# Compressed keys' block sums: plain 4 KB gathers through the shared ring, added on chip, in place of 1 KB gathers that add in SBUF

## The chip, the cores and the metric

The kernel runs on one core of a Trainium2 chip. Its time is device microseconds of one launch, from start to end, and a version is judged by the median of its runs. The engines are TensorE (PE, with its weight load PEld), VectorE (DVE), ScalarE (ACT), GpSimd (POOL) and SyncE (SP, which here only issues DMAs). DMA moves data on 16 engines that share the queues of SP and POOL.

## What is computed

One step of a two-layer decoder (model width 1024) for a prompt of 512 tokens and for 8 samples of one token each. The samples look back on 2048 cached tokens, which lie in pages of 128 rows, in an order that a page table gives. Each layer has a mixer and a squared-ReLU feed-forward (1024 to 4096 and back); all weights are shared by prompt and samples. The mixer has three groups of heads: forgetting attention ("fox"), native sparse attention ("NSA") and a multi-scale pooling.

The change is in the samples' compressed branch of NSA. It takes the means of the cached k_cmp and v_cmp over blocks of 64 rows, scores the query against the 32 means, and those scores also select the blocks that the selected branch reads next. A row of this cache holds four vectors, of which the branch needs the first two: 256 of 512 floats.

```
cache_nsa_kv (DEPTH, N_POOL_PAGES, PAGE_SIZE, 4, KV_NSA, HEAD_DIM)   # [k_cmp, v_cmp, k_sel, v_sel]

def _cmp_branch(q5, qpos, kc_rows, vc_rows):
    def blocks(r):                                   # CMP_BLOCK = 64
        rb = r[:, :nbc * CMP_BLOCK].reshape(b, nbc, CMP_BLOCK, KV_NSA, HEAD_DIM)
        return jnp.mean(rb.astype(f32), axis=2).astype(r.dtype)
    kc, vc = blocks(kc_rows), blocks(vc_rows)
    s = jnp.einsum('btkgd,bnkd->btkgn', q5, kc) * SCALE
    ...
    p = _masked_softmax(s, mask)
    o = jnp.einsum('btkgn,bnkd->btkgd', p.astype(vc.dtype), vc)
    return o, jnp.sum(p, axis=3)                     # the sum ranks the blocks to select
```

There are 8 samples x 32 blocks = 256 blocks in each layer, two halves of 128 blocks. One block lies on one partition.

## The kernel before

**How work is put in order.** The program is written as chains, Python generators that emit a piece of work at a time and say what it weighs. `merge` (L118) always takes the chain that is furthest behind, by emitted weight over the chain's total (`W_G`, `W_S`, `W_C0`, `W_C1` and so on, L26). A chain that waits for another's result steps aside. Then the Tile framework's scheduler gives each engine a fixed order of instructions when the program is built, by priorities and by the order of emission. On the chip an engine goes through its order and cannot pass an instruction that waits.

**The main chain.** `main` (L1522) goes through each layer's dense products, all by `next_gemm`: a product of a 128 x 128 weight tile with up to 512 columns of activations is done as three fp32r products, hi x hi, hi x lo and lo x hi (`pg`, L336). Weights come as 256 KB tiles `wr` through SP and are split in `wh` and `wl` by ACT and DVE. The feed-forward runs in NC = 8 chunks, each with four tiles of ff1 and eight of ff2. Chunks 0 to 3 hold the prompt's columns alone. Chunks 4 to 7 are joint: their columns hold the samples too, and they are emitted only once the samples' chain is "joined".

**The samples' chain.** `sample` (L1466) goes first through the fox heads: per layer 64 gathers `fk` of 768 KB, on POOL's queue, each multiplied by the queries (L1204), summed, and multiplied with the weights on PE (`pvf`, L1212). Then `key_sample`, a unit per sample, gathers window keys `kt` and selected keys `st`: `psb` (L1122) are its small products, `pvw` and `pvs` (L1418) those with the values. The selected rows come from `ixs`, which `nsa_sample` (L1294) works out after it has waited for `kct`, the transposed means. Then `rows_of` multiplies the samples' rows by whole weight rows, `wrow` tiles of 512 KB through SP, four `prw` products (L268) each: 8 tiles of the output projection, then for SQ = 2 quarters 8 tiles of ff1 and 8 of ff2, 40 in all. Between them stand the samples' norms (`psr`). After the last of these rows comes "joined".

**The ring.** `ring` (L180) gives big tiles out of one rotation of RING = 5 buffers of 768 KB, in order of emission. `fk`, `kt`, `st` and `wrow` go through it. A tile's load can start when the fifth tile before it has been read. `take` (L1161) loads up to five ahead.

**The compressed sums.** `pre_cmp` (L631) sums while it gathers. For each half g and each row r of 64, one indirect DMA on POOL's queue brings 256 floats (1 KB) for each of 128 blocks, and from the third row on it adds them to what stands in SBUF (`compute_op` add). Two accumulators a half (CA = 2) take turns:

```
L637  G.indirect_dma_start(out=ys[g][r % CA], out_offset=None, in_=nsav,
                           in_offset=bass.IndirectOffsetOnAxis(ap=idxc[:, l, g:g + 1], axis=0),
                           element_offset=r * 512, compute_op=OP.bypass if r < CA else OP.add)
```

These 128 tiles `cg` a layer have buffers of their own. Then DVE adds the two accumulators and scales, PE transposes (`pkc`), and `kct` is there. Layer 0's sums are the chain `cmp0`, from the start of the layer, beside the mixer. Layer 1's are emitted during layer 0 by `fill` (L1640) once layer 0's NSA samples are done.

Of the kernel before, what the change touches and what calls it, by code (L numbers as in the profile page):

```python
# [34 lines left out]
def constants():  # L35
# [44 lines left out]
    c["ph"], c["p64"], c["p8"], c["p8x8"] = 128.0 * (p % 2)[:, None], 2.0 * (p % 64)[:, None], (p % 8)[:, None], 8.0 * (p % 8)[:, None]  # L80
# [57 lines left out]
def trunk(ctx: ExitStack, tc: tile.TileContext, x_prompt, x_sample, cache_fox_kv, cache_fox_logf, cache_nsa_kv,  # L138
# [44 lines left out]
    # ---------------------------------------------------------------- weight stream  # L183
# [15 lines left out]
    # the output projection in two halves: the features that come first, then the NSA heads'  # L199
# [64 lines left out]
    def row_mm(acc, rows, k, hk, raw, first, last):  # L264
        """A weight tile of 128 rows, 512 columns times up to 32 rows of activations, fp32."""
        for c in range(2 * hk, 2 * hk + 2):
          with PF():
            PE.matmul(acc[c * 32:(c + 1) * 32, 0:256], rows[:, k, :], raw[:, (c % 2) * 256:(c % 2 + 1) * 256],  # L268
                      start=first, stop=last)

    def row_end(sb, tag):
        """The sums feature-major: [128, f, c, 32] holds feature tile 2 c + f."""
# [8 lines left out]
    def ada(l, parts, tag, raws=None, hold=True):  # L281
        """Parts of a layer's modulation, from c's columns; hold: a PSUM bank is held for all of a part's tiles."""
# [27 lines left out]
    def next_gemm(kind, mhi, mlo, evac, cols, tag="g"):  # L310
        """The stream's next weight tile times the given ranges of columns."""
# [7 lines left out]
        for o in range(2 if two else 1):  # L319
            nk = 4 if two else 8  # L320
            for a, b in cols:
                acc = ps("pg", tag)
                if it[2] == "fg":
                    # 24 outputs alone, in fp32: a quarter of the features to each column group
# [18 lines left out]
    # ---------------------------------------------------------------- x and c  # L343
# [20 lines left out]
    # the first two parts' weights in what is free at the start  # L364
# [41 lines left out]
    # ---------------------------------------------------------------- vectors  # L406
# [21 lines left out]
    # ---------------------------------------------------------------- constants on chip  # L428
# [24 lines left out]
    # ---------------------------------------------------------------- page indices  # L453
# [5 lines left out]
    for l in range(L):  # L459
        t = ring("ti", (128, 2))  # L460
        V.tensor_copy(t, pgc)
        V.tensor_scalar(t, t, 256.0, C("ph"), op0=OP.mult, op1=OP.add)
        V.tensor_scalar(idxc[:, l], t, float(l * NPOOL * 256), None, op0=OP.add)
# [14 lines left out]
    nsav = cache_nsa_kv.rearrange("l n r (t2 t) k d -> (l n r t2) (t k d)", t2=2)  # L478

# [4 lines left out]
    # ---------------------------------------------------------------- norms  # L484
# [9 lines left out]
    def squares(X, fresh=None, then=None):  # L494
        """The prompt's squares of X summed over the features, on all partitions. fresh(k) brings tile k up to date, and
        then(k) reads it."""
# [11 lines left out]
    def pre_scaled(l, X, gi, sp, bp, fresh, tag, ph=None):  # L508
        """The prompt's X * g * (1 + scale), split, and 1 / rms(X), which is left for the products to take. The shift is
        the operand's column T (and the next, as these are even in number). ph: the squares, if they are there."""  # L510
# [27 lines left out]
    def post_norm(X, O, acc, pool=True):  # L538
        """The update X += rms(O) tile by tile, for O with its gates and acc the squares summed over the feature tiles."""
# [19 lines left out]
    def gated(O, gg, acc, m, src, a, b):  # L559
        """Columns a..b of O's tile m: the squares of src into acc, src times its gates to O."""  # L560
# [11 lines left out]
    def s_rms(x):  # L572
        """1 / rms of the samples' columns x [128, 8, 8], on all partitions."""
# [8 lines left out]
    def s_post(l, gi, gp, x):  # L582
        """XS += rms(x) * g * gate."""
# [8 lines left out]
    def s_pre(l, gi, sp, bp, out, rs=None):  # L592
        """out = rms(XS) * g * (1 + scale) + shift."""
# [9 lines left out]
    def s_put(hi, lo, x):  # L603
        """The samples' columns of an operand."""
# [7 lines left out]
    # ---------------------------------------------------------------- what a layer's samples need of the caches alone  # L612
# [18 lines left out]
    def pre_cmp(l):  # L631
# [35 lines left out]
    def layer(l, X, hi, lo, rsw):  # L667
# [972 lines left out]
        def fill():  # L1640
# [4 lines left out]
            for _ in pre_cmp(l + 1):  # L1645
                yield 0.25
# [81 lines left out]
```

## Time and profile before

| | |
|---|---|
| runs, us | 2087.47, 2085.21, 2074.53 |
| median, us | 2085.21 |
| profiled execution, span, us | 2088.8 |
| its mean granted clock of TensorE | 0.903 |

The profile is of one execution. Its span runs from the first instruction to the last, and the page gives no launch time beside it, so that the span stands for that execution's time. It lies 3.6 us above the median of the three runs, which is no more than they differ from each other.

The page shows each engine's busy time as a sum over the span and in 40 slices of 52.2 us. "PE 1888.1 (90%) x13848" is busy time, share of the span and number of instructions. Below are three rows of the 40 slices, in tenths: POOL's busy share, the clock that TensorE was granted, and the busy share of the 16 DMA engines.

```profile
POOL 0788888878888887100000254553435455000000
PEclk9998985696988888999999999975789999999998
DMA  8988888876988867786334666653337466684332
```

Slices 1 to 11 are layer 0's mixer, 12 to 21 its feed-forward, 22 to 31 layer 1's mixer and 32 to 40 its feed-forward. POOL is nearly full up to the 16th slice, in the middle of layer 0's feed-forward, and then idle until layer 1's mixer. DMA is near 0.8 as long, and about half as busy in layer 1's mixer.

A group row of the page reads: line, engine, operation, out<-in by the program's names (partitions x elements), number of instructions | busy time in us, mean of one in ns | idle time of the engine just before them, and what ended most of it.

### The profile page before, as it was taken

What the parts mean: (1) busy time and instruction counts of PE and PEld (TensorE: products, weight loads), DVE (VectorE), ACT (ScalarE), POOL (GpSimd) and SP (SyncE); (2) the same over time, 40 slices, a digit from 0 to 9 for tenths busy, and PEclk for the clock granted to TensorE, in tenths of its full rate; (3) what the DMA queues carried; (4) which work ended last, traced back from release to release, by engine and by line L of the source; (5) the groups of instructions that cost most, each with busy time, mean ns of one, the idle gap of its engine ahead of it and who ended that gap; (6) DMA issues with size and microseconds to landing.
All of it is one profiled execution on the core that took longest, in us unless ns stands there. A gap on an engine that the chain in (4) does not pass through costs nothing. (4 is left out here: it accounts for less than half of the span.)

```text
span 2088.8 us, 37062 instructions
## 1 busy us (share of the span) xinstructions
PE 1888.1 (90%) x13848; PEld 1475.4 (71%) x13848; DVE 1253.2 (60%) x3064; ACT 856.8 (41%) x1994; POOL 946.5 (45%) x670
## 2 busy tenths in 40 slices
PE   6987976998876888999998999979998989999998
PEld 3866753465545678779996777755665778879998
DVE  3557665665573357634557668786557967534555
ACT  3333332455442223323446344344555533324445
POOL 0788888878888887100000254553435455000000
PEclk9998985696988888999999999975789999999998
DMA  8988888876988867786334666653337466684332
GB/s 285 277 200 226 218 202 226 222 216 110 263 208 199 218 165 194 245 296 213 92 92 127 180 218 201 206 168 126 115 107 233 138 183 182 194 279 140 89 90 77
DMA packets 333687, 387.42 MB, mean 185 GB/s; under 512 B 30489, under 2 KB 267771, under 8 KB 333364
## 3 DMA queue, kind: packets, MB, share of 16 engines
q1 hardware_dynamic: 272324, 233.24, 36.4%
q0 software_dynamic: 61184, 151.82, 27.8%
q8 instruction: 110, 1.80, 0.4%
q14 instruction: 69, 0.57, 0.1%
HBM read 363.71 MB, written 21.44 MB: 184 GB/s over the span
## 5 line engine op out<-in xcount | busy, mean ns | idle before, releaser
L336 PE MATMUL pg<-ah,wh 128*128 128x262 f32 (+4 forms) x1792 | 549.4, 308 | 32.1 <-DVE rl L1570 9.7
L336 PE MATMUL pg<-ah,wl 128*128 128x262 f32 (+4 forms) x1792 | 544.0, 304 | 8.6 <-DVE wl L245 6.8
L336 PE MATMUL pg<-al,wh 128*128 128x262 f32 (+4 forms) x1792 | 544.1, 305 | 4.7 <-DVE al L522 4.5
L637 POOL DMA_INDIRECT cg<-in_cache_nsa_kv_dram,idxc x256 | 423.6, 1655 | 88.4 <-issue 68.9
L178 ACT ACTIVATE wh<-wr 128x512 fp32r<-128x512 f32 x372 | 234.0, 630 | 458.1 <-PE pg L336 416.5
L336 PEld LDWEIGHTS pg<-ah,wh 128*128 128x128 f32 x1792 | 351.4, 197 | 58.8 <-issue 32.5
L336 PE MATMUL pg<-a,wh 128*128 128x262 f32 (+3 forms) x1664 | 380.5, 317 | 11.6 <-DVE F L1589 7.0
L336 PEld LDWEIGHTS pg<-ah,wl 128*128 128x128 f32 x1792 | 351.9, 196 | 29.3 <-issue 11.6
L336 PEld LDWEIGHTS pg<-al,wh 128*128 128x128 f32 x1792 | 350.6, 196 | 28.4 <-issue 11.0
L245 DVE TENSOR_TENSOR wl<-wr,wh 128x512 fp32r<-128x512 f32 x368 | 276.2, 751 | 130.0 <-ACT wh L178 127.0
L336 PEld LDWEIGHTS pg<-a,wh 128*128 128x128 f32 x1664 | 278.2, 192 | 41.4 <-DVE F L1589 10.8
L336 PE MATMUL pg<-a,wl 128*128 128x258 f32 (+3 forms) x832 | 260.6, 314 | 0.9 <-DVE wl L245 0.9
L481 POOL DMA_INDIRECT fk<-in_cache_fox_kv_dram,idxf x128 | 131.8, 1030 | 276.7 <-PE pvf L1212 114.8
L1204 POOL TENSOR_TENSOR fk<-fk,qb 128x768 f32<-128x768 f32 x96 | 186.5, 1961 | 118.4 <-DMA fk<-in_cache_fox_kv_dram,idxf 58.1
L336 PEld LDWEIGHTS pg<-a,wl 128*128 128x128 f32 x832 | 160.0, 192 | 8.9 <-DVE wl L245 1.4
L1589 DVE TENSOR_TENSOR F<-F,pg 128x262 f32<-128x262 f32 (+3 forms) x188 | 88.3, 474 | 113.7 <-PE pg L336 108.7
L1205 DVE TENSOR_REDUCE S<-fk 128x12 f32<-128x768 f32 x128 | 120.6, 944 | 43.9 <-POOL fk L1204 43.4
L1626 POOL TENSOR_TENSOR xt<-xt,yt 128x512 f32<-128x512 f32 x2 | 2.5, 1266 | 308.6 <-DVE xt L1628 307.3
L268 PE MATMUL pada<-wa,cT 128*32 128x256 f32 x640 | 97.5, 432 | 41.8 <-DMA wa<-in_w_ada_dram 32.1
L481 POOL DMA_INDIRECT st<-in_cache_nsa_kv_dram,ixs x96 | 102.2, 1065 | 72.3 <-PE pvs L1418 25.9
L1571 ACT ACTIVATE rl<-rl,wb 128x256 f32<-128x256 f32 (+2 forms) x128 | 64.2, 505 | 119.5 <-DVE rl L1570 119.2
L178 ACT ACTIVATE P<-P,st 128x128 f32<-128x128 f32 (+3 forms) x144 | 79.2, 558 | 64.8 <-DVE st L869 38.4
(435 smaller groups left out, 2820.7 us busy)
## 6 DMA issues: line engine op xcount, KB each, us to landing
wr<-in_w_ff_dram SPq DMA_DIRECT2D x256, 256.0 KB
wa<-in_w_ada_dram SPq DMA_DIRECT2D x160, 256.0 KB
wrow<-in_w_ff_dram SPq DMA_DIRECT2D x64, 512.0 KB
wr<-in_w_in_dram SPq DMA_DIRECT2D x80, 256.0 KB
out_dram<-kt SPq DMA_DIRECT2D x16, 512.0 KB
wrow<-in_w_out_dram SPq DMA_DIRECT2D x16, 512.0 KB
kt<-in_cache_nsa_win_dram SPq DMA_DIRECT2D x16, 448.0 KB
qb<-qscr SPq DMA_DIRECT2D x32, 192.0 KB
```

The costliest lines, as they stand in the source:

```text
L178: return S.activation(out, in_, AF.Copy, scale=scale)
L245: V.tensor_tensor(lo, raw, hi.bitcast(F32), op=OP.subtract)
L268: PE.matmul(acc[c * 32:(c + 1) * 32, 0:256], rows[:, k, :], raw[:, (c % 2) * 256:(c % 2 + 1) * 256], start=first, stop=last)
L336: PE.matmul(acc[:, 0:b - a], wt, x(k)[:, a:b], start=n == 0, stop=n == 3 * nk - 1)
L481: G.indirect_dma_start(out=out, out_offset=None, in_=view, in_offset=bass.IndirectOffsetOnAxis(ap=idx, axis=0))
L637: G.indirect_dma_start(out=ys[g][r % CA], out_offset=None, in_=nsav, in_offset=bass.IndirectOffsetOnAxis(ap=idxc[:, l, g:g + 1], axis=0), ...
L1204: (G if i == 0 or l else V).tensor_tensor(kk, kk, qb[b][:, None, :].to_broadcast([128, 2, 384]), op=OP.mult)
L1205: V.tensor_reduce(S4[:, 2 * i:2 * i + 2], kk.rearrange("p r (h d) -> p r h d", d=64), axis=AX, op=OP.add)
L1571: S.activation(r[:, a:e], r[:, a:e], AF.Relu, bias=st["wb"])
L1589: V.tensor_tensor(F[:, m, a:b], F[:, m, a:b], p[:, 0:b - a], op=OP.add)
L1626: G.tensor_tensor(xt[:, b, h], xt[:, b, h], t, op=OP.add)
```

## The change

Gathers of whole rows take the place of the 1 KB gathers, and the sum is made by an engine. `nsa2` views the cache with two rows to an element, so one index and an offset reach 2 rows of 512 floats, 4 KB for each block. A gather is now a plain copy into a ring tile `cr` of 512 KB, half of which (k_sel and v_sel) is not used. For each layer there are 64 of them (32 row pairs, 2 halves) in place of 128. VectorE (layer 0) or GpSimd (layer 1) copies the first pair's 2 x 256 floats to `cg` and adds each later one. At the end the two rows of `cg` are added. While layer 0's means are not there, `take` loads only three tiles ahead in place of five. The chains' weight is 0.5 a gather in place of 0.25, with half as many.

```diff
-    c["ph"], ... = 128.0 * (p % 2)[:, None], ...
+    c["ph"], ... = 32.0 * (p % 2)[:, None], ...
...
-        V.tensor_scalar(t, t, 256.0, C("ph"), op0=OP.mult, op1=OP.add)
-        V.tensor_scalar(idxc[:, l], t, float(l * NPOOL * 256), None, op0=OP.add)
+        V.tensor_scalar(t, t, 64.0, C("ph"), op0=OP.mult, op1=OP.add)
+        V.tensor_scalar(idxc[:, l], t, float(l * NPOOL * 64), None, op0=OP.add)
...
+    nsa2 = cache_nsa_kv.rearrange("l n (s r) t k d -> (l n s) (r t k d)", r=2)
...
-    def pre_cmp(l):
+    def pre_cmp(l, room=lambda: True):
...
-        ys = [[wk.tile([128, 256], F32, name="cg", bufs=2 * CA) for _ in range(CA)] for g in range(2)]
-        for r in range(64):
+        eng = G if l else V
+        ys = [wk.tile([128, 2, 256], F32, name="cg", bufs=2) for g in range(2)]
+        for r in range(32):
             for g in range(2):
-                G.indirect_dma_start(out=ys[g][r % CA], out_offset=None, in_=nsav,
+                while not room():
+                    yield None
+                x = ring("cr", (128, 1024))
+                G.indirect_dma_start(out=x, out_offset=None, in_=nsa2,
                                      in_offset=bass.IndirectOffsetOnAxis(ap=idxc[:, l, g:g + 1], axis=0),
-                                     element_offset=r * 512, compute_op=OP.bypass if r < CA else OP.add)
+                                     element_offset=r * 1024)
+                x = x.rearrange("p (r c) -> p r c", r=2)[:, :, 0:256]
+                if r == 0:
+                    eng.tensor_copy(ys[g], x)
+                else:
+                    eng.tensor_tensor(ys[g], ys[g], x, op=OP.add)
                 yield
         kvc = []
         for g in range(2):
-            for i in range(1, CA):
-                V.tensor_tensor(ys[g][0], ys[g][0], ys[g][i], op=OP.add)
+            V.tensor_tensor(ys[g][:, 0], ys[g][:, 0], ys[g][:, 1], op=OP.add)
...
+        def cmp_done():
+            return l > 0 or "kct" in pre[0]
...
-            while feed["n"] < min(u + RING, len(loads)):
+            while feed["n"] < min(u + (RING if cmp_done() else RING - 2), len(loads)):
...
             for _ in pre_cmp(l + 1):
-                yield 0.25
+                yield 0.5
...
             for _ in pre_cmp(0):
-                yield 0.25
+                yield 0.5
```

The `room` argument is always true here. Comments and docstrings are taken out, which moves line numbers only.

Since the ring's order and the chains' pace set the engines' orders, the change moves work that it does not touch. Line numbers after the change are higher by about 14 from the ring on. First PE's order of before, where the samples' weight rows begin in layer 0 (`prw` from `wrow`, among the prompt's feed-forward products `pg`; `pob` is the NSA samples' last transposes, x4 means four instructions in a row):

```order
L336 MATMUL pg_8385<-al_5706,wh_8276 128x256
L268 MATMUL prw_7678<-wrow_7679,catp_291 32x256 x4
L268 MATMUL prw_7678<-wrow_7726,catp_291 32x256 x4
L268 MATMUL prw_7678<-wrow_7813,catp_291 32x256 x4
L1436 MATMUL pob_7508<-cst1_72,aw_6934 64x12 x4
L1436 MATMUL pob_7508<-cst1_72,aw_7468 64x12 x4
L336 MATMUL pg_8486<-ah_5705,wh_8344 128x256
L336 MATMUL pg_8486<-ah_5705,wl_8345 128x256
L336 MATMUL pg_8552<-ah_5705,wh_8445 128x258
```

The rows stand between products of an early prompt-only chunk's ff1 and more `pg` of the prompt-only chunks follow. After the change, PE's order at the end of chunk 3, the last of the four prompt-only ones:

```order
L336 MATMUL pg_9055<-a2_8400,wl_8977 128x512
L336 MATMUL pg_9055<-a2_8401,wh_8976 128x512
L1132 MATMUL psb_7417<-S4_7405,cst0_70 128x24
L1133 MATMUL psb_7417<-cst0_70,nmN_6448 128x24
L1128 MATMUL pmx_7489<-cst0_70,mx_7487 6x128
L1432 MATMUL pvw_7116<-kt_7126,pads2_277 32x64 x8
L1132 MATMUL psb_7492<-S4_7478,cst0_70 128x24
L1133 MATMUL psb_7492<-cst0_70,nmN_6448 128x24
L1432 MATMUL pvs_7235<-kt_7126,pads2_277 32x64 x2
L1432 MATMUL pvs_7235<-st_7269,pads2_277 32x64 x6
```

The last `pg` of the four chunks now stands ahead of the last samples' key units (`psb`, `pvw`, `pvs`), which no `pg` follows any more. Further on in that order, from the output projection's rows to chunk 4's first product:

```order
L268 MATMUL prw_7823<-wrow_7987,catp_291 32x256 x4
L627 MATMUL ptt_7858<-tt_7856,cst1_72 128x48
L268 MATMUL prw_7823<-wrow_8075,catp_291 32x256 x4
L268 MATMUL prw_7823<-wrow_8091,catp_291 32x256 x4
L268 MATMUL prw_7823<-wrow_8168,catp_291 32x256 x4
L275 MATMUL pmod_8179<-cst0_70,rowsb_8177 128x128 x2
L580 MATMUL psr_8189<-ssr_8187,cst0_70 128x8
L580 MATMUL psr_8251<-ssr_8249,cst0_70 128x8
L336 MATMUL pg_9201<-ah_5767,wh_9033 128x260
```

The output projection's rows, the samples' two norms (`psr`) and then chunk 4's first `pg` stand one behind the other; the names' numbers count the order of emission, and the gaps between the `wrow` numbers hold other work, `cr` tiles among it. The ff2 rows of the samples' first quarter, on PE, before:

```order
L336 MATMUL pg<-a_8338,wl 128x512
L336 MATMUL pg<-a_8339,wh 128x512
L268 MATMUL prw<-wrow,hp 32x256 x20
L336 MATMUL pg<-a_8332,wh 128x512
L336 MATMUL pg<-a_8332,wl 128x512
L336 MATMUL pg<-a_8333,wh 128x512
```

and after:

```order
L336 MATMUL pg<-a_9187,wl 128x258
L336 MATMUL pg<-a_9188,wh 128x258
L268 MATMUL prw<-wrow,hp 32x256 x32
L275 MATMUL pmod<-cst_70,rowsb 128x128 x2
L268 MATMUL prw<-wrow,catp 32x256 x32
```

Before, twenty `prw` (five `wrow` tiles) stood between two `pg` of a prompt-only chunk. Now 32 stand in a row, then another quarter's 32 of ff1, and behind the rows shown another 32 of ff2: 96 products, 24 `wrow` tiles, with no `pg` between. Last, POOL's order at the place where layer 1's gathers begin; before:

```order
L481 DMA st_6655<-in_cache_nsa_kv_dram,ixs_6212 128x256 x6
L481 DMA kt_6664<-in_cache_nsa_kv_dram,ixs_6212 128x256 x2
L637 DMA cg_7722<-in_cache_nsa_kv_dram,idxc_299 128x256
L637 DMA cg_7721<-in_cache_nsa_kv_dram,idxc_299 128x256
L637 DMA cg_7723<-in_cache_nsa_kv_dram,idxc_299 128x256
L637 DMA cg_7720<-in_cache_nsa_kv_dram,idxc_299 128x256
L1404 TENSOR_TENSOR prod_6831<-kt_6502,qb_6653 128x768
```

and after:

```order
L482 DMA st_7396<-in_cache_nsa_kv_dram,ixs_6278 128x256 x6
L1418 TENSOR_TENSOR prod_7510<-kt_7278,qb_7394 128x768
L643 DMA cr_7867<-in_cache_nsa_kv_dram,idxc_299 128x1024
L648 COPY cg_7865<-cr_7867 128x512
L643 DMA cr_7880<-in_cache_nsa_kv_dram,idxc_299 128x1024
L482 DMA lf_7830<-in_cache_fox_logf_dram,idxl_301 128x96 x8
L648 COPY cg_7866<-cr_7880 128x512
```

Layer 1's gathers stood among the samples' key gathers of layer 0, in buffers of their own. Now they stand behind the last of those, at the place of the `wrow` loads, and take turns with these in the ring.

More of the change, by code (lines that the diff above doesn't have):

```diff
@@ L79, in constants @@
     c["cv"], c["cn"] = cv.reshape(128, 32), ((cv - 1.0) * BIG).reshape(128, 32)
-    c["ph"], c["p64"], c["p8"], c["p8x8"] = 128.0 * (p % 2)[:, None], 2.0 * (p % 64)[:, None], (p % 8)[:, None], 8.0 * (p % 8)[:, None]
+    c["ph"], c["p64"], c["p8"], c["p8x8"] = 32.0 * (p % 2)[:, None], 2.0 * (p % 64)[:, None], (p % 8)[:, None], 8.0 * (p % 8)[:, None]
     c["smask"] = np.where((np.arange(4)[None, :] == 3) & (p[:, None] > 64), -BIG, 0.0)
@@ L642, in pre_cmp @@
         for g in range(2):
-            for i in range(1, CA):
-                V.tensor_tensor(ys[g][0], ys[g][0], ys[g][i], op=OP.add)
+            V.tensor_tensor(ys[g][:, 0], ys[g][:, 0], ys[g][:, 1], op=OP.add)
             y = wk.tile([128, 256], F32, name="kvc", bufs=2)
-            V.tensor_scalar(y, ys[g][0], 1.0 / 64, None, op0=OP.mult)
+            V.tensor_scalar(y, ys[g][:, 0], 1.0 / 64, None, op0=OP.mult)
             kvc.append(y)
```

## Prediction

> **What bounds the kernel now.** I read the page's first part, then the windows by stage, then who PE waits for. The page and the stages (columns: start:end, length, busy time and instructions of PE, weight load, DVE, ACT, POOL, granted clock, DMA share, GB/s):
>
> ```profile
> span 2088.8 us, 37062 instructions
> PE 1888.1 (90%) x13848; PEld 1475.4 (71%) x13848; DVE 1253.2 (60%) x3064; ACT 856.8 (41%) x1994; POOL 946.5 (45%) x670
> ...
> core 0: us, PE busy (x) PEld busy (x) DVE busy (x) ACT busy (x) POOL busy (x), PEclk, DMA share, GB/s
> 49.00:591.00 542.00, 465.93 (x3144) 325.17 (x3146) 336.91 (x906) 218.69 (x538) 448.75 (x301) 0.84 0.85 219
> 591.00:860.00 269.00, 221.15 (x1573) 176.13 (x1564) 151.12 (x327) 82.44 (x181) 206.62 (x146) 0.88 0.76 191
> 1138.00:1613.00 475.00, 444.75 (x3061) 313.42 (x3061) 322.34 (x815) 216.76 (x537) 200.87 (x139) 0.88 0.54 173
> 1613.00:1794.00 181.00, 167.77 (x1291) 145.00 (x1292) 137.99 (x283) 75.12 (x167) 80.72 (x71) 0.92 0.58 170
> ```
>
> PE bounds the whole (90%). The first two windows are layer 0's mixer and the start of its feed-forward; the last two are the same stages of layer 1, where no compressed gather runs. Layer 0's mixer leaves PE idle for 542 - 466 = 76 us, layer 1's for 475 - 445 = 30 us. So the gathers can have cost at most about 46 us of idle PE in the mixer. The rest of layer 0's excess is modulation work.
>
> Now the change's own lines, and what PE waits for between 591 and 860:
>
> ```profile
> L637 POOL DMA_INDIRECT cg<-in_cache_nsa_kv_dram,idxc x256 | 423.6, 1655 | 88.4 <-issue 68.9 <-DVE idxc L463 7.4 <-DMA cg<-in_cache_nsa_kv_dram,idxc 4.5
> L481 POOL DMA_INDIRECT fk<-in_cache_fox_kv_dram,idxf x128 | 131.8, 1030 | 276.7 <-PE pvf L1212 114.8 <-PE prw L268 94.8 <-issue 20.7
> L913 POOL TENSOR_TENSOR al<-zn,ah 128x512 fp32r<-128x512 f32 x5 | 6.0, 1213 | 9.3 <-ACT ah L178 7.3 <-PE psS L852 2.0
> ...
> L245 DVE TENSOR_TENSOR wl<-wr,wh 128x512 fp32r<-128x512 f32 x368 | 276.2, 751 | 130.0 <-ACT wh L178 127.0 <-DMA kt<-in_cache_nsa_win_dram 0.2
> ...
> PE pada L268 <- DMA wa<-in_w_ada_dram: 22.4, 8, 10.3
> ```
>
> The gathers hold POOL for 424 us, and PE hardly waits for POOL at all: its one long wait there is for modulation weights.
>
> **The change, part by part.** *POOL.* 256 accumulating gathers of 1655 ns (423.6 us) go. 128 plain ones come; the nearest row is fk, plain and 768 KB, at 1030 ns: 132 us. Layer 1's 64 additions (two of them copies) at about 1.21 us (128x512 on POOL, L913) are 78 us. POOL falls from 424 to about 210 us. That is off the path, so it is worth nothing by itself.
>
> *DVE.* Layer 0's 64 additions at 751 ns (128x512, L245) are 48 us more on an engine that is 337 of 542 us busy. An addition also waits in order for its rows to land. The nearest row, from the waits of DVE in 49:591, is the forgetting heads' multiplication:
>
> ```profile
> DVE fk L1204 <- DMA fk<-in_cache_fox_kv_dram,idxf: 67.2, 15, 13.7
> ```
>
> 32 multiplications waited 67 us, 2.1 us each; 64 additions at that are 134 us. Work and waits fill 182 of DVE's 205 free microseconds. If a quarter of that reached PE, the mixer would lose 46 us. If POOL and DMA were what held PE, it would gain the 46 us of above. Neither end is nearer, so I take 0 for the mixer and keep -46 and +46.
>
> *DMA bytes.* What is read in all, and `cg` alone in layer 0's mixer:
>
> ```profile
> HBM read 363.71 MB, written 21.44 MB: 184 GB/s over the span
> ...
> 49.00:591.00 542.00, 1.36 (x4) 310.14 (x193) 0.84 0.85 219
> ```
>
> 256 x 128 KB become 128 x 512 KB: 33.6 MB more of 363.7 MB read. In layer 0's mixer it is a wash (64 x 512 KB, 34 MB, for the some 190 x 128 KB, 25 MB, that ran there). In layer 1's share it is not: those 33.6 MB now run beside the samples' weight rows, next.
>
> *The ring, where the price is.* The new tiles take turns in a ring of five with the forgetting heads' tiles (layer 0) and with `wrow`, the samples' weight rows (layer 1's share). The order rows shown above say what that does. In the old order PE mixes the 160 `prw` products (40 `wrow` tiles) into the `pg` products. In the new order all `pg` of the four prompt-only chunks come first. Then stand some 2.5 of the 8 samples' key units, the 8 `wrow` tiles of the output projection, and only then chunk 4's first `pg`. After its ff1 come 24 `wrow` tiles with no `pg` between. By emission numbers about 50 of layer 1's 64 `cr` tiles stand in the ring among those 40 `wrow`. Before, the same place looks like this (windows of `pg` alone, then all engines, then `prw` alone; 1216 records and four times 312 or so are the products up to chunk 4):
>
> ```profile
> 0.00:578.90 578.90, 204.01 (x1216) 170.64 (x1216) 25.00 (x85) 6.10 (x17) 0.85 0.85 223
> 578.90:701.40 122.50, 56.64 (x312) 45.81 (x313) 4.14 (x13) 4.40 (x9) 0.85 0.81 199
> 847.10:918.70 71.60, 51.88 (x313) 43.23 (x314) 9.37 (x22) 0.00 (x0) 1.00 0.82 273
> 918.70:958.20 39.50, 30.16 (x218) 27.16 (x216) 4.69 (x14) 0.63 (x4) 1.00 0.92 330
> ...
> 578.90:918.70 339.80, 287.27 (x2146) 224.98 (x2145) 192.58 (x438) 105.22 (x231) 216.08 (x151) 0.89 0.78 210
> 918.70:958.20 39.50, 39.33 (x376) 31.50 (x374) 14.34 (x37) 17.24 (x41) 4.68 (x5) 1.00 0.92 330
> ...
> 578.90:918.70 339.80, 10.72 (x168) 4.65 (x168) 0.77 (x2) 0.89 0.78 210
> ```
>
> So PE is through the four chunks at 918.7, and through the last row product 39.5 us later, never idle.
>
> *PE reaches that point earlier.* What moves behind it: 10.7 us of `prw`, and 2.5 of 8 samples' `psb` (10.3 us in all, next fence): 3 us. Idle there is 339.8 - 287.3 = 52.5 us; at layer 1's rate (13.2 us in 181) the remaining 286 us hold 21: 32 us less, since the gathers leave this window and with them the load beside `wa`. Together -46 us (without the idle, -14).
>
> *Then it waits.* Rows for the pieces: key units of eight samples (`psb`, layer 0 and layer 1), what POOL does for them, the hops between row products and the norms of the samples (chain of waits), bare `pg` at full clock:
>
> ```profile
> 683.00:860.00 177.00, 10.35 (x60) 9.62 (x60) 2.90 (x15) 0.90 0.73 189
> 1660.00:1795.00 135.00, 10.31 (x62) 9.33 (x61) 3.04 (x16) 0.95 0.60 175
> ...
> L481 POOL DMA_INDIRECT st<-in_cache_nsa_kv_dram,ixs x96 | 102.2, 1065 | 72.3 <-PE pvs L1418 25.9 <-issue 23.8 <-DMA qb<-qscr 17.7
> L481 POOL DMA_INDIRECT kt<-in_cache_nsa_kv_dram,ixs x32 | 31.6, 986 | 9.6 <-issue 7.8 <-PE psb L1123 0.3 <-DMA wr<-in_w_ff_dram 0.3
> L1404 POOL TENSOR_TENSOR prod<-kt,qb 128x768 f32<-128x768 f32 x16 | 32.9, 2056 | 22.5 <-issue 22.2 <-DVE S L1408 0.2
> ...
> 1817.68 2.94 PE pg L336 x23
> 1820.61 0.22 PE pmod L275 x2
> ...
> 1824.82 0.12 PE psr L579 x2
> ...
> 1829.46 0.12 PE psr L579 x2
> ...
> 1910.75 46.41 PE pg L336 x381
> ```
>
> - 2.5 samples at 16.9 us (135/8), or at POOL's 10.4 us (six st and two kt gathers, 6 x 1.065 + 2 x 0.986, and a product, 2.06): 26 to 42, I take 35.
> - A tile of 512 KB takes 1.59 us at 330 GB/s (918:958, the fastest stretch) and 2.74 us at 191 GB/s (591:860). The rows are bare, so I take 1.7, near the fast end. Output projection: 8 `wrow` and 8 `cr`, two loaded ahead: 14 tiles, 24 us (22 to 38).
> - Two norms of the samples, 4.6 us from `psr` to `psr` with the same again around them: 12 us (8 to 14).
> - Chunk 4's ff1: 192 `pg` at 0.122 us are 23 us, 16 tiles are 27: 28 us (23 to 44).
> - 24 bare `wrow` with some 26 `cr`: 50 tiles, 85 us (80 to 137), and 5 us (0 to 9) for hops of 2.9 us that loads run under.
>
> Sum 189 us (159 to 284) in place of 39.5: +150 (+120 to +245). Behind SP's blocked `wrow` stand chunk 4's later weights, but PE's order needs them no sooner. The last 14 `cr` end about when the next mean is transposed: +5 (0 to +10).
>
> **A rule against the change.** The granted clock falls where PE idles, and not only there:
>
> ```profile
> 1400.00:1500.00 100.00, 93.19 (x448) 54.85 (x447) 66.92 (x153) 46.13 (x134) 46.42 (x33) 0.64 0.38 129
> 2075.00:2088.80 13.80, 5.43 (x29) 3.94 (x29) 4.93 (x9) 4.08 (x10) 2.53 (x2) 0.59 0.43 155
> ```
>
> The end, with PE 39% busy, has 0.59; the stretch from 1400, 93% busy, has 0.64. In the bare stretch PE would be busy for a third of the time, so at half clock chunk 4's 192 `pg` take 47 us in place of 28: +19. The Trainium skill, TensorE: Matmul & The Clock Gate, "Part 1: The HAM clock gate", says that PE falls to half clock after an idle window of some 3.4 us and comes back after a busy one. By that rule the sum is 19 us higher, and the first row above says that busy share alone doesn't decide.
>
> **Sum.** 0 - 46 + 150 + 5 = +109 on the profiled execution's span of 2088.8: 2198. The profile gives no time around its span; the runs' median, 2085.2, lies 3.6 below that span, which I carry over: 2194.
>
> **Rivals.**
> - *The chain is bare, as summed:* 2194, some 2140 to 2250. For it: the order is fixed, PE can't pass those rows.
> - *The ring also stalls layer 0's mixer:* a pair of forgetting tiles finds fewer loads ahead, since layer 0's `cr` take turns with them, and PE meets `pvf` early. The mixer's upper end, +46, and slow tiles (+35): 2275. For it, the 2.1 us that DVE waits per tile now; against it, a DMA share in the mixer that should fall below 0.85.
> - *Half clock in the bare stretch:* 2213, by the two rows above.
> - *Faster:* the mixer gains its 46 us, and its clock goes from 0.84 to layer 1's 0.88 (466 us x 0.04/0.88 = 21). With -46 after it, the bare stretch may then take 152 us before the gain is gone. At 130 us (tiles near 1.3 us) the time is 2088.8 - 67 - 46 + 90 - 3.6 = 2062. Against it: my lower bound is 159 us.
> - *No change:* the same gains with the lower bound of 159 us: 2088.8 - 113 + 120 + 0 - 3.6 = 2092.
>
> **Chances.** Bare chain 0.62, mixer stalled too 0.15, half clock 0.07, faster 0.08, no change 0.08. A measurement tells about 1% (21 us) from no change: faster 0.08, same 0.08, slower 0.84. The range 2105 to 2290 leaves out the last two rivals and little above.
>
> **What would show it.** Right: POOL's gather group near 130 us at 1.0 us each; between the fourth and fifth chunk PE idles for over 100 us, waiting for `wrow` and for the samples' chain; that chain, not `pg`, leads up to about 1060. PE reaches the 2432nd product before 900. DMA in the bare stretch near 300 GB/s. Wrong: `pg` idle there under 60 us, or tiles far from 1.7 us; a mixer that ends 40 us sooner or later than 591; waits of DVE for `cr` over 100 us, which would make the second rival the cause.

## The result, and the profile after

| | kernel before | kernel after |
|---|---|---|
| runs | 4, 2074.53 to 2087.47 us | 4, 2099.69 to 2115.66 us |
| median, us | 2085.78 | 2103.17 |
| profiled span, us | 2088.8 | 2099.3 |

The ratio is 1.0109, with a 95% interval of 1.0074 to 1.0143. The kernel got slower, as forecast, but by 17 us (1.1%) and not by 109; 2103 also lies below the range given. The page of the kernel after begins (busy time and instructions by engine, then two of the rows of 40 slices and the bytes):

```profile
span 2099.3 us, 37161 instructions
PE 1868.3 (89%) x13848; PEld 1454.9 (69%) x13848; DVE 1314.4 (63%) x3128; ACT 855.5 (41%) x1994; POOL 739.4 (35%) x606
...
POOL 0434443433304656777000353554425255000000
PEclk9999968979999985858999999977889999999999
...
HBM read 397.26 MB, written 21.44 MB: 199 GB/s over the span
...
L643 POOL DMA_INDIRECT cr<-in_cache_nsa_kv_dram,idxc x128 | 129.6, 1013 | 152.0 <-PE pvf L1226 46.6 <-PE prw L268 18.1 <-PE pada L268 16.1
```

POOL, nearly full up to the 16th slice before, is about half as busy now, and the reads are the 33.6 MB more. To see where the time went, count PE's dense products `pg` and note when the n-th begins (the count leaves out 32 of layer 0's 64 small products for the gates, so the 1184th is the 1216th `pg` record of the trace, and so on). The 1184th is the end of layer 0's mixer, the 2432nd the last of the four prompt-only chunks, the 2720th stands behind nearly all the samples' rows, and the 3968th ends layer 0 (all in us):

| | 1184th | 2432nd | 2720th | 3968th | end |
|---|---|---|---|---|---|
| before | 578.8 | 918.6 | 967.0 | 1120.4 | 2088.8 |
| after | 509.1 | 768.4 | 960.4 | 1117.2 | 2099.3 |

PE is 70 us earlier at the end of the mixer and 150 us earlier after the four chunks. It gives back 144 us in the next 288 products (192.0 us in place of 48.4) and 3 us in chunks 5 to 7. The change is a draw at the end of layer 0. The windows by stage (columns as before), first the kernel before, then two stretches of the kernel after, then its stretch from 768 to 960 in five pieces:

```profile
49.00:578.80 529.80, 458.40 (x3071) 320.61 (x3071) 324.90 (x885) 215.16 (x531) 439.28 (x295) 0.84 0.85 218
```

```profile
48.60:509.10 460.50, 427.82 (x3032) 303.28 (x3033) 336.11 (x914) 210.92 (x523) 179.94 (x152) 0.89 0.75 249
509.10:768.40 259.30, 247.31 (x1836) 199.67 (x1835) 190.72 (x399) 103.97 (x225) 106.75 (x89) 0.99 0.68 210
768.40:792.80 24.40, 14.96 (x123) 7.72 (x125) 9.81 (x21) 1.85 (x7) 16.95 (x16) 0.58 0.75 248
792.80:819.00 26.20, 13.16 (x116) 4.63 (x116) 11.99 (x32) 0.77 (x2) 15.82 (x16) 0.57 0.90 314
819.00:834.00 15.00, 4.65 (x19) 4.12 (x20) 8.95 (x16) 0.95 (x4) 12.07 (x11) 0.50 0.71 227
834.00:862.30 28.30, 28.30 (x236) 24.08 (x236) 14.45 (x25) 13.41 (x32) 21.17 (x18) 0.95 0.96 332
862.30:960.40 98.10, 42.83 (x307) 20.49 (x305) 10.93 (x23) 5.29 (x11) 73.02 (x67) 0.58 0.91 321
```

Up to the 2432nd product, PE's idle time falls from 71.4 + 52.5 to 32.7 + 12.0 us, by 79 us; busy time falls by 71. About half of these 71 is work that moved behind (10.7 us of `prw`, 13 of `pada`, 11 of the samples' smaller products: 35), but the same dense products alone take 398 us in place of 424, at a granted clock of 0.89 and 0.99 in place of 0.84 and 0.89. The last five rows are the bare stretch: key units, the output projection's rows, the norms, chunk 4's ff1 (at a clock of 0.95) and the 24 bare `wrow` tiles; ff1 begins at 831 and ends at 869, a few us outside its row.

Why was PE late before? The waits of POOL in the mixer, a view that the prediction does not show, point at a cause, which e1 and e9 below test (engine, line, what it waited for: total, times, longest). Before:

```profile
POOL cg L637 <- issue: 50.4, 176, 0.3
POOL fk L481 <- issue: 12.3, 39, 1.2
POOL cg L637 <- DVE idxc L463: 7.4, 1, 7.4
POOL cg L637 <- DMA cg<-in_cache_nsa_kv_dram,idxc: 4.2, 3, 3.2
```

and after:

```profile
POOL fk L1218 <- DMA fk<-in_cache_fox_kv_dram,idxf: 64.1, 19, 6.8
POOL fk L482 <- DVE cg L650: 60.5, 16, 15.9
POOL cr L643 <- PE pvf L1226: 46.6, 11, 13.6
```

Before, POOL was busy for 439 of 530 us, and 63 us of the other 91 were the issue ahead of its gathers, mostly 0.3 us each. It hardly waited for another engine: POOL's queue was nearly full. After the change it waits for transfers, for DVE and for PE. In the Trainium skill, Perfetto Trace Analysis, "Identifying the Most-Contended Engine" and "Optimization Strategy" say that occupancy tells the bottleneck for GpSimd and that the busiest engine can change from regime to regime. The row of the kernel before's mixer agrees with that only if issue is added: POOL's 83% there is below PE's 87%, with the issue it is 95%.

### The profile page after: what moved, and what is told of

Its sections match the earlier page's. It is cut to its first block, busy times and chain, and to the rows that moved or that the text cites. A ratio compares the mean times of both kernels' runs of the same rounds, so it can differ in the third digit from the quotient of the medians.

```text
span 2099.3 us, 37161 instructions
## 1 busy us (share of the span) xinstructions
PE 1868.3 (89%) x13848; PEld 1454.9 (69%) x13848; DVE 1314.4 (63%) x3128; ACT 855.5 (41%) x1994; POOL 739.4 (35%) x606
## 5 line engine op out<-in xcount | busy, mean ns | idle before, releaser
L336 PE MATMUL pg<-ah,wl 128*128 128x262 f32 (+4 forms) x1792 | 538.6, 301 | 5.2 <-DVE wl L245 2.8
L245 DVE TENSOR_TENSOR wl<-wr,wh 128x512 fp32r<-128x512 f32 x368 | 292.5, 795 | 140.1 <-ACT wh L178 126.2
L643 POOL DMA_INDIRECT cr<-in_cache_nsa_kv_dram,idxc x128 | 129.6, 1013 | 152.0 <-PE pvf L1226 46.6
L1603 DVE TENSOR_TENSOR F<-F,pg 128x262 f32<-128x262 f32 (+3 forms) x188 | 87.8, 473 | 99.5 <-PE pg L336 94.9
## 6 DMA issues: line engine op xcount, KB each, us to landing
qb<-qscr SPq DMA_DIRECT2D x32, 192.0 KB
```

What stands on the lines that cost most here:

```text
L245: V.tensor_tensor(lo, raw, hi.bitcast(F32), op=OP.subtract)
L336: PE.matmul(acc[:, 0:b - a], wt, x(k)[:, a:b], start=n == 0, stop=n == 3 * nk - 1)
L643: G.indirect_dma_start(out=x, out_offset=None, in_=nsa2, in_offset=bass.IndirectOffsetOnAxis(ap=idxc[:, l, g:g + 1], axis=0), element_offs ...
L1603: V.tensor_tensor(F[:, m, a:b], F[:, m, a:b], p[:, 0:b - a], op=OP.add)
```

## The experiments

The numbers below are ratios to the kernel before, run beside each, with 95% intervals, and times of the n-th product from the profiles, in us. For e9 to e14 the kernel before ran at 2123 us, so their times are some 2% late beside the others. The sums are left out, in whole or in part, in e1, e5, e6 and e9.

| | ratio | 1184th | 2432nd | 2720th | 3968th | end |
|---|---|---|---|---|---|---|
| e1_old_plain | 0.958 (0.953 to 0.962) | 509.8 | 824.0 | 872.4 | 1025.2 | 1976.4 |
| e2_layer0_only | 1.028 (1.024 to 1.032) | 517.1 | 834.5 | 1011.3 | 1163.6 | 2124.6 |
| e3_gate | 0.980 (0.975 to 0.986) | 515.5 | 772.8 | 882.2 | 1071.6 | 2036.1 |
| e4_gate_fast0 | 0.972 (0.968 to 0.976) | 555.3 | 843.1 | 902.5 | 1075.9 | 2010.4 |
| e5_plain_poolfill | 0.976 (0.968 to 0.985) | 529.3 | 830.5 | 931.3 | 1083.5 | 2042.8 |
| e6_old_half | 1.000 (0.996 to 1.004) | 580.9 | 919.5 | 966.7 | 1119.0 | 2078.3 |
| e7_fast0 | 0.989 (0.982 to 0.997) | 558.6 | 846.7 | 959.0 | 1115.0 | 2062.2 |
| e8_private | 0.988 (0.978 to 0.999) | 587.7 | 881.4 | 936.0 | 1091.7 | 2052.2 |
| e9_old_tiny | 1.019 (1.013 to 1.025) | 594.0 | 946.0 | 1006.5 | 1158.8 | 2147.9 |
| e10_gate_v100 | 0.972 (0.967 to 0.978) | 576.2 | 881.5 | 938.3 | 1091.9 | 2056.3 |
| e11_gate_v140 | 0.969 (0.965 to 0.973) | 567.0 | 868.8 | 926.3 | 1080.9 | 2046.9 |
| e12_old_fkV | 0.984 (0.980 to 0.988) | 589.0 | 917.3 | 964.6 | 1116.9 | 2081.7 |
| e13_gate80 | 0.982 (0.976 to 0.987) | 588.1 | 887.8 | 942.4 | 1112.6 | 2084.7 |
| e14_gate80_v | 0.982 (0.974 to 0.990) | 592.1 | 893.8 | 940.0 | 1095.1 | 2079.2 |

### What the adding gathers cost: e1, e6, e9

The theories were POOL's time for a gather, the adding transfers' load on DMA, and the other order of instructions. e1 takes the adding away and nothing else; e6 and e9 leave it and shrink what is moved, with a view, an index and zeros in the rest of the tile to match.

```diff
# e1, in the kernel before
-    element_offset=r * 512, compute_op=OP.bypass if r < CA else OP.add)
+    element_offset=r * 512, compute_op=OP.bypass)
# e6 (e9: 16 floats in place of 128)
-    G.indirect_dma_start(out=ys[g][r % CA], ...
+    G.indirect_dma_start(out=ys[g][r % CA][:, 0:128], ...
```

> The kernel before, with its 256 compressed gathers plain instead of adding (the sum of the block's rows is left out, each accumulator keeps the last row). Same order of instructions, same bytes. If it was POOL's queue that held layer 0 (a gather of 1.655 us each time), a plain gather falls to about 1.03 us like the fk gathers, POOL is relieved of 256 x 0.62 = 160 us, PE reaches the 2432nd pg product near 845 instead of 919, and the time is 2015 to 2050. If the gain of the changed kernel came from its other order of instructions, or from the place of the work, the time stays at 2086 within 10 us though the gathers get shorter. If the gathers stay at 1.65 us, the adding isn't what makes them long.

> The kernel before, with adding gathers of 128 floats (512 B) instead of 256: the values' sums are left out. As many gathers with as many rows for POOL to describe, half the bytes for DMA; nearly the old order. If POOL's time holds layer 0, a gather stays near 1.6 us, the 1184th product comes at 565 to 580 and the time at 2070 to 2090. If the adding transfers' load on the DMA engines holds it, that load falls by up to half, the product comes at 520 to 550 and the time below 2050.

> The kernel before, with adding gathers of 16 floats (64 B) instead of 256; the other columns' sums are left out. POOL still issues 256 adding gathers, DMA has next to nothing of them to move, and the order is nearly the old one. If it is only POOL's time for an adding gather (1.63 to 1.66 us, against 1.09 for a plain one) that held layer 0, the 1184th product comes at 565 to 585 and the time is 2065 to 2090, as with the kernel before. If anything in the transfers held it (load, or an addition's way to memory and back), the product comes before 540 and the time falls below 2040. e5, in which POOL was filled by another instruction, gave 529 and could not tell, since the fill did not stand behind the gathers in POOL's order.

The order of PE in e1 is row for row that of the kernel before. The gathers' groups in e1, e6 and e9 (1 KB plain, 512 B adding, 64 B adding; busy time and mean ns of one come first behind the bar):

```profile
L637 POOL DMA_INDIRECT cg<-in_cache_nsa_kv_dram,idxc x256 | 277.8, 1085 | 95.0 <-issue 66.9
```

```profile
L642 POOL DMA_INDIRECT cg<-in_cache_nsa_kv_dram,idxc x256 | 416.2, 1626 | 84.5 <-issue 67.2 <-DVE idxc L463 8.0 <-DMA cg<-in_cache_nsa_kv_dram,idxc 3.0
```

```profile
L642 POOL DMA_INDIRECT cg<-in_cache_nsa_kv_dram,idxc x256 | 418.0, 1633 | 81.2 <-issue 68.6 <-DVE idxc L463 8.3 <-DVE st L872 0.9
```

An adding gather holds POOL for 1.63 to 1.66 us whether it brings 64 B or 1 KB for each block; a plain one takes 1.09. In e6 the 1184th product comes at 581 and the time is that of the kernel before, near its first expectation. The mixer's windows in e1 and in e9:

```profile
47.00:509.80 462.80, 438.23 (x3069) 307.06 (x3070) 328.52 (x880) 213.69 (x527) 329.33 (x295) 0.88 0.76 247
```

```profile
49.00:594.00 545.00, 460.22 (x3081) 321.24 (x3081) 313.62 (x891) 212.82 (x531) 439.00 (x298) 0.85 0.61 170
```

In e9 the DMA share falls from 0.85 to 0.61, and yet the mixer takes 545 us; the 530 us of before would be 540 on that chip, where all is some 2% slower. In e1 the share falls to 0.76, POOL falls by 110 us and the mixer by 67. How a full POOL queue reaches PE stands in DVE's waits in the mixer: the forgetting heads' tiles `fk` are gathered, and some of them multiplied, in that same queue, and DVE waits for both. In the kernel before, then in e1, then in e9:

```profile
DVE fk L1204 <- DMA fk<-in_cache_fox_kv_dram,idxf: 67.2, 15, 13.7
DVE S L1205 <- POOL fk L1204: 18.3, 7, 3.8
```

```profile
DVE fk L1204 <- DMA fk<-in_cache_fox_kv_dram,idxf: 10.6, 7, 3.1
```

```profile
DVE fk L1209 <- DMA fk<-in_cache_fox_kv_dram,idxf: 67.9, 17, 10.0
DVE S L1210 <- POOL fk L1209: 33.1, 10, 5.8
```

All of PE's waits for DVE in the mixer sum to 55 us before, 19 in e1 and 54 in e9. So the load of the transfers did not hold layer 0; POOL's time for adding gathers did, and it came to PE through DVE. In the old order, that alone is worth 95 us at the 2432nd product (69 of them in the mixer, 26 behind it), and 4.2% of the kernel's time (1989 beside 2076 us, less than the 2015 to 2050 expected). Of the other 55 us by which the kernel after is early there, some 35 match the work that moved behind; the rest was not separated. Why e9 is 1.9% slower than the kernel before was not found.

### Tries on POOL that could not tell: e5, e12

```diff
# e5: e1, and behind each gather
+    G.tensor_tensor(dmy, dmy, dmy, op=OP.mult)
# e12, in the kernel before
-    (G if i == 0 or l else V).tensor_tensor(kk, ...
+    (G if l else V).tensor_tensor(kk, ...
```

> As e1_old_plain, with a GpSimd multiplication of 128x256 on a tile of its own behind each plain gather (about 0.6 us, half of what 128x512 took), so that POOL spends about as long on a gather as it did with the adding ones, while the DMA engines have the plain ones' load. If it is POOL's time that held the mixer, the 1184th pg product (510 us in e1, 579 before) comes at 555 to 580 again. If it is what the adding costs the DMA engines, it stays at 510 to 525. The order behind the mixer is not the old one (key units and 11 weight-row tiles stand bare), so the whole time, 2010 to 2090, tells less than that product.

> The kernel before, adding gathers and all, with layer 0's forgetting multiplications all on VectorE (32 of 64 were on GpSimd, about 1.96 us each, 63 us of POOL; on VectorE they take 0.96 us). If POOL's queue bounds layer 0's mixer (it waited there for nothing but its own issue), the 1184th product comes 35 to 60 us earlier than with the kernel before on this chip, at 520 to 545 for a chip like the first, and the time falls by 30 to 60 us. If POOL only seems full, VectorE's 31 us more and its waits make it no earlier: 570 to 600, and no gain.

In both the order of instructions came out another. In e5 POOL was busy for 345 us of the mixer, and not for 439, since only 76 of the 256 fills and 161 gathers stood there, where e1 had 190 gathers; the product came at 529, between the two expectations. In e12 POOL's 63 us were filled up again: 228 adding gathers ran ahead of the 1184th product, where 190 had.

```profile
49.00:589.00 540.00, 451.52 (x3056) 313.55 (x3055) 306.38 (x908) 212.85 (x527) 441.09 (x300) 0.86 0.88 217
```

POOL is at 441 us as before, and the mixer no shorter, against the first expectation. The 1.6% gained came later; its source was not found. Neither refutes a full POOL queue; neither shows it by itself.

### What made the bare stretch long: e2, e3, e7, e4

```diff
# e2: layer 0 by the new gathers, layer 1 by the old ones
# e3, in the kernel after (fill)
-            while "nsa_s" not in ready:
+            while "joined" not in ready:
# e7: W_C0 70 -> 140 (layer 0's gathers at twice the pace);  e4: e3 and e7
```

> Layer 0's sums as after the change, layer 1's as before (1 KB gathers that add, no ring tiles). If layer 0's gathers alone made the early arrival, PE is through the mixer near 520 as after the change and reaches the 2432nd product between 768 and 800. If the old gathers of layer 1 in the feed-forward held PE too, it comes at 830 to 860. The bare stretch behind it has no cr tiles in the ring: the key units, 13 wrow tiles and two norms, some 80 to 100 us instead of 192. Time 2030 to 2060 if both hold; near 2100 if the stretch is long because of the late samples' chain and not because of cr in the ring.

> After the change, with layer 1's gathers emitted only when the samples' weight rows of layer 0 are done (fill waits for joined). If the ring's turns with cr made the bare stretch long, PE's waits for wrow in it fall from 60 us to under 20 and the time to 2030 to 2050. If the samples' chain is late whatever the ring does, the rows stay bare and the time falls by under 25 us, to 2080 or so.

> After the change, with W_C0 140 alone (layer 0's gathers at twice the pace; layer 1's still take turns with the weight rows). It completes the square with the kernel after (2103 beside 2086) and e3_gate, e4_gate_fast0 (2037 and 2021 beside 2076). If the ring's turns cost what e3 gained (66 us) also when the rows stand among pg products, the time is 2065 to 2085; if rows among pg products hide the longer loads, it is 2015 to 2035.

> As e3_gate, and layer 0's gathers are emitted at twice the pace (W_C0 140 instead of 70), so that the means, the key units and the rows come earlier; in PE's order all 40 weight-row tiles then stand among the products of the prompt-only chunks. If the bare stretch is the only price, it goes: rows end near the 2455th product, and the time is 1950 to 2000. If faster gathers starve the forgetting heads' tiles in the ring, the mixer ends 30 to 50 us later than 520 and the time is 2000 to 2050.

With layer 1's gathers out of the way (e3) the 288 products from the 2432nd take 109 us in place of 192, and PE's wait for `wrow` in `w_ff` falls from 52.2 to 5.3 us. PE's order moved along: of the 24 `wrow` tiles that stood bare behind chunk 4's ff1 only 8 still do, and the others stand among chunk 4's products. So the 83 us are the price of `cr` in the ring's order, the turns and the bare place together. The other 61 us over the 48 of the kernel before stay without any `cr` among the rows: for 46 us, from 773 to 819, key units, rows and norms still stand ahead of chunk 4. The two edits make a square of ratios: 1.011 without either, 0.980 gated, 0.989 with the pace, 0.972 with both. The two gains overlap; that rows among `pg` products hide the longer loads would explain it, but was not tried by itself, and in e7 17 of the 40 tiles still stand bare, up to 948 us. With the faster pace the mixer ends at 555 us and not at 516, as the second expectation of e4 said; e13 below speaks against its reason.

e2 is the miss: slower than both its expectations. Its bare stretch has no `cr` in the ring and still takes 177 us. POOL there, from 825 to 1008 us:

```profile
L643 POOL DMA_INDIRECT cg<-in_cache_nsa_kv_dram,idxc x48 | 74.7, 1556 | 16.1 <-issue 12.2 <-DMA cg<-in_cache_nsa_kv_dram,idxc 3.9
L484 POOL DMA_INDIRECT st<-in_cache_nsa_kv_dram,ixs x12 | 12.4, 1034 | 3.5 <-issue 2.9 <-DMA out_dram<-kt 0.3 <-DMA wa<-in_w_ada_dram 0.3
```

Layer 1's 48 adding gathers stand in POOL's queue among the key units' gathers. The key units take 61 us (834.5 to 896), where the kernel after has 24; but some three and a half stand bare there in place of two, so that the order has a part in it that was not separated. The four prompt-only chunks ahead, through which the other 80 gathers ran, were 58 us longer than after the change (517 to 834 us against 509 to 768). That is not the adding alone: in e1, in the old order, plain gathers made this part shorter by 26 us (314 in place of 340).

### Who adds: e10, e11, e8

In e3 the chunks 5 to 7 lost time: 189 us from the 2720th to the 3968th product, where the kernel before took 153. e11 is e4 with one change, VectorE adding for layer 1; e10 has W_C0 100 as well. e8 leaves the ring: plain 1 KB gathers into three buffers of their own, all added by VectorE.

```diff
# e10, e11
-        eng = G if l else V
+        eng = V
# e8
+    x = wk.tile([128, 256], F32, name="cr", bufs=3) if r else ys[g]
+    G.indirect_dma_start(out=x, ..., element_offset=r * 512)
+    if r:
+        V.tensor_tensor(ys[g], ys[g], x, op=OP.add)
```

> As e4_gate_fast0, with two things changed: layer 1's additions on VectorE instead of GpSimd, and W_C0 100 instead of 140. In e3 VectorE's split of a weight tile took 1.49 us beside GpSimd's additions in chunks 4 to 7, against 0.69 in the kernel before, and those chunks took 190 us instead of 153. If GpSimd's additions did that, the split is back at 0.7 to 0.8 us, the chunks take 155 to 165 us, and the time is 1975 to 2005 where e4 had 2021 beside 2076. If it was the gathers' traffic and not the additions, it stays near 1.4 us and the time at 2010 to 2030.

> As e4_gate_fast0 (W_C0 140), with layer 1's additions on VectorE: the one change. If GpSimd's additions slowed VectorE, the time falls from 2021 by 15 to 35 us; if not, it stays within 10 us or rises by VectorE's 44 us more.

> Neither kernel's way: plain gathers of 1 KB as in e1, into three 1 KB buffers of their own, added by VectorE to one sum for each half, with W_C0 100. The sums are whole again. If plain gathers outside the ring are what counts, the time is that of e1 (1989 beside 2076) plus some of 254 additions of about 0.4 us on DVE, 1985 to 2015. If three buffers are too few and POOL's queue blocks on additions, it is over 2040.

VectorE's split of a weight tile in chunks 5 to 7, in e3 and then in e11:

```profile
L245 DVE TENSOR_TENSOR wl<-wr,wh 128x512 fp32r<-128x512 f32 x52 | 77.5, 1491 | 21.9 <-ACT wh L178 21.8
L1603 DVE TENSOR_TENSOR F<-F,pg 128x262 f32<-128x262 f32 x28 | 11.9, 424 | 8.2 <-PE pg L336 7.7
...
L650 POOL TENSOR_TENSOR cg<-cg,cr 128x512 f32<-128x512 f32 x62 | 79.5, 1293 | 0.9
```

```profile
L245 DVE TENSOR_TENSOR wl<-wr,wh 128x512 fp32r<-128x512 f32 x52 | 35.9, 691 | 24.3 <-ACT wh L178 20.6 <-issue 2.9 <-ACT a L1589 0.7
```

Beside GpSimd's additions the split takes twice its time; with the additions on VectorE it is back at 0.69 us, though 45 gathers still run there, and the three chunks at 155 us. So it was the additions and not the gathers' traffic. The whole time hardly follows: 0.969 against 0.972 with overlapping intervals, and POOL now waits 46.6 us there for VectorE's additions before its next gathers, which may be why. e8's plain gathers were POOL's 1.08 us, but POOL waited 78 us for additions, and VectorE 83 us for tiles to land: three buffers are too few, and the mixer ended at 588.

### Both at once: e13, e14

> As e4_gate_fast0 (gated, additions as in the change) with W_C0 80: in PE's order the rows end at the 2396th product, before chunk 4. If layer 0's pace at 140 cost the mixer its 40 us (1184th product 555 against 516 in e3), this slower pace gives back half: ratio to before 0.955 to 0.968. If not, 0.97 to 0.98.

> As e13_gate80 with layer 1's additions on VectorE. By e11 against e4 this is worth under 1% either way: within 10 us of e13, while chunks 5 to 7 (2816th to 3968th product) take 143 us instead of some 160.

W_C0 80 in e3's and e10's kernels did not do it: 0.982 in both. The mixer of e13 ended at 588 us, some 577 without that chip's 2%, later than with 140 (555) and with 70 (516). So the pace does not set that end in the way of e4's expectation; what does was not found. The best versions that compute the whole are e11, e4 and e10, 3.1%, 2.8% and 2.8% faster than the kernel before, with intervals that overlap. e14's chunks 5 to 7 took 144 us from the 2816th product, e13's 157, as expected.

### Where the 1% lies: e15 to e18

> The changed kernel once more. In its first profile it left layer 0 3 us ahead of the kernel before (3968th product at 1117 against 1120 us) and lost 13 us in layer 1, where the two orders hardly differ. If layer 1's loss belongs to the change, layer 1 (from the 3970th product to the end) takes 8 to 20 us longer here too than in e16 and e18. If it is the spread of single executions, the sign or size changes.

> The kernel before once more, beside e15 and e17: layer 1 some 953 us in its first profile. The 1184th product at 579, the 2432nd at 919 us, a few per cent later where all is slower.

> The changed kernel, third profile. As e15: 8 to 20 us more in layer 1 than e16 and e18 if the loss belongs to the change, else another sign or size.

> The kernel before, third profile. As e16: layer 1 near 953 us; its difference from e16 shows how far single executions of one kernel differ there.

| | 1184th | 2432nd | 3968th | from the 3970th to the end |
|---|---|---|---|---|
| before, three profiles | 579, 571, 575 | 919, 915, 916 | 1120, 1116, 1116 | 953, 949, 956 |
| after, three profiles | 509, 519, 510 | 768, 776, 771 | 1117, 1131, 1116 | 966, 972, 955 |

Beside a kernel before at 2083 us, the kernel after stood at 1.014 (0.994 to 1.034) in e15 and 1.015 (0.994 to 1.035) in e17, two runs each, from 2089 to 2122 us; the kernel before stood at 1.000 in both e16 and e18. The early arrival is there each time, and layer 0 ends even within 4 us on the mean (1121 against 1117). Layer 1 is some 12 us longer on the mean, 964.2 against 952.7, but one of three executions of the kernel after lies within those of the kernel before. e1, with the old order row for row, took 935 us there. So layer 1's time differs by this much without any change in its own instructions, and whether the change has a part in its 12 us, and with it the cause of the 1% itself, stays open.

## Why the prediction was wrong, step by step

- **The direction** was right. The size was not: 17 us in place of 109, and where these 17 lie stays open, as layer 0, which the whole sum is about, ended even.
- **"PE reaches that point earlier", -46 us, is the step that failed:** it measured -150. Behind it stands "POOL falls ... off the path, so it is worth nothing by itself" and "I take 0 for the mixer". The page was read for whom PE waits for, and PE waits for DVE. DVE's 67.2 us of waits for `fk` tiles were read as what loads cost; that these loads stood behind adding gathers in POOL's queue was not asked. With plain gathers and nothing else changed (e1) they are 10.6 us, and PE is 95 us earlier. The mixer ended 70 us sooner, beyond even the -46 end of the range, since that end counted idle time alone; this was one of the prediction's own signs of being wrong. The work that moved behind, put at 14 us, was 35.
- **The clock** was left out of the sum and named only in the rival "faster", at 21 us. It rose from 0.84 to 0.89 in the mixer and from 0.89 to 0.99 behind it, and the dense products took 25 us less.
- **"Then it waits", 189 us in place of 39.5:** right in mechanism and near in size. From the 2432nd product to the end of the bare rows passed 182 us. The pieces, forecast and measured: key units 35 and 24 (two stood bare, not 2.5); output projection's rows 24 and 26; norms 12 and 12; chunk 4's ff1 28 and 38; bare rows 90 and 82. That the sum is so near is in part luck: 11 us too much for the key units stand against 10 too few for ff1.
- **Tiles of 1.7 us:** 0.52 MB at the 321 GB/s of the last piece are 1.63.
- **POOL from 424 to about 210 us:** 129.6 for the gathers and 79.1 for the additions, 209 in all. Right.
- **DVE:** 64 additions as 48 us were 43; their waits for rows, put at 134 us, were 22. The price had been taken from tiles that waited for a full POOL queue. What had not been counted is GpSimd's additions beside VectorE: the split at 0.90 us in chunks 5 to 7 in place of 0.69. Those chunks took 3 us longer than before.
- **Half clock in the bare stretch:** the granted clock was 0.50 to 0.58 in its idle pieces, but chunk 4's ff1 ran at 0.95 and took 10 us more than forecast, not 19.
- **The rival "no change"** came nearest. It had this mechanism, mixer and clock gaining against the stretch, with 113 us of gain against 120; it measured 150 against 147 by the end of layer 0. Its 2092 is near because both of its terms were some 30 us too small. It was given 0.08.

## What to carry to other kernels

An engine that PE never waits for can still set PE's pace through the engine between them: look for one whose idle time is mostly issue, and ask who waits for it in turn. A wait for a load can be a wait for the queue that the load is issued from. Where a change frees such an engine, count the clock with the idle time. A resource that two streams share by order of emission is costed by where that order puts them; moving one stream's start (one line, e3) was worth 3% here, more than the change itself moved.

## What was not expected of the hardware

- An adding gather of 128 rows cost POOL 1.60 to 1.66 us on the mean, a plain one of the same rows 1.00 to 1.09 us. The bytes made little difference: adding, 1.63 us with 64 B a row and 1.66 with 1 KB; plain, 1.09 with 1 KB (e1) and 1.01 with 4 KB (the kernel after).
- The plain 1 KB gathers of e1 went over DMA in 4 KB packets (7,936 more of these than before, of some 0.2 us), the adding ones in 1 KB packets (31,744 of 0.11 us): 16 engines' time of some 100 us in place of 218. Reading four times the bytes by 4 KB rows, as the change does, took about 190.
- Beside GpSimd's additions VectorE's subtraction of two tiles in SBUF took 1.49 us in place of 0.69, while the additions of a PSUM tile to an SBUF one (L1603) stayed at 0.42 us. The Trainium skill, SBUF — State Buffer, "SBUF: two separate sides", says that GpSimd shares a pair of ports with VectorE's operations that have two inputs in SBUF, and that the loser waits for the whole instruction. Both rows agree with it in which operation is held up; that the wait lasts a whole instruction no row here shows.
